# More block pairs by seven products in a decoder trunk, with weight sums made in DRAM by accumulating DMAs

## The chip, the cores and the metric

The kernel runs on one core of a Trainium2 chip. TensorE (PE) multiplies and adds up in PSUM; ScalarE (ACT), VectorE (DVE) and GpSimd (POOL) do elementwise work; SyncE (SP) issues DMAs, and ACT and POOL can issue them too. Sixteen DMA engines carry every transfer of the core. The metric is the device time of one execution in microseconds (us); lower is better.

## The reference

Everything is float32: a trunk of two layers over 256 tokens with a model width of 2048. Layer 0 is a retention mixer with eight heads, layer 1 a block-sparse attention with a relative position bias; a gated MLP with a causal convolution of width 3 follows each. Cut to what matters:

```python
for i in range(2):
    hn = rms_norm(h, mix_norm[i])
    if i == 0:                         # retention
        q, k, v, g = split(hn @ w_in)  # w_in 2048 x 12288: q, k 8 x 256, v, g 8 x 512
        ...
        h = h + (silu(g) * group_norm(o)) @ w_out      # 4096 x 2048
    else:                              # attention, T5 bias
        q, k, v = split(hn @ w_qkv)                    # 2048 x 6144
        h = h + attention(q, k, v) @ w_out             # 2048 x 2048
    u = causal_conv(rms_norm(h, ffn_norm[i]) @ w_up)   # 2048 x 11264
    gate, val = split(u)
    h = h + (silu(gate) * val) @ w_down                # 5632 x 2048
out = rms_norm(h, final_norm)
```

## The kernel before

**Precision.** A float32 value is kept as two parts of PE's faster float32 format, a high part and the rest. A product of two such values takes three matmuls: high by high, high by rest, rest by high. Activations stand transposed in SBUF, both parts side by side (hT, yT, oT, actT). Weights come from DRAM as float32 (tile raw, four buffers of 1 MB) and are split on the chip: ACT copies the high part to wh (L226), DVE subtracts to get the rest, wl (L227). wh and wl have four buffers each, of 1024 columns.

**Panels.** A list of "halves" is built first, and then run in order (`run`, `step`). A half is one split and the matmuls that use it. Before half i runs, the splits up to half i + 3 are issued (`LOOKAHEAD`), and the loads of raw up to two units beyond that (`issue_split`, `issue_dma`, on SP's queue). PE, ACT and DVE follow this program order; SP and POOL have their own. `panel_b` makes 256 columns transposed (q, k and the up projections): a unit of 1 MB is two halves. `panel_s` (L365) makes 1024 columns by pairs of 128 rows of the weight: a pair is a 2 x 2 block matrix, 256 tokens by 256 rows times 256 rows by 1024 columns, and one unit of 1 MB.

**Pairs by eight and by seven.** `eight` (L480) takes a pair as eight block products, which are 24 matmuls of 512 columns in two halves. `seven` (L450) takes it in the Strassen-Winograd form: seven products, 21 matmuls, in four halves of 6, 3, 6 and 6. It needs four sums of activation blocks ("forms") and four sums of weight blocks. The weight's sums are made by DVE in raw, in place, between the splits:

```python
def split_b11_b22(raw, wh, wl):          # L239
    b = blocks(raw)
    split_to(blocks(wh), blocks(wl), b[:, 0:4:3, :])
    dve.tensor_tensor(b[:, 0:2, :], b[:, 0:4:3, :], b[:, 1:2, :].to_broadcast([P, 2, 512]), op=ALU.add)
```

and `split_b21` (L244) adds two sums of 512 columns (L247, L248). The forms of a pair of the down projection are made in the up projection (`forms`, L1014), stored to DRAM (tile f, L1021) and fetched by ACT's queue (L440) into a slot of hT, eight slots in all; on arrival they are split by ACT and DVE (L445, L446). In the heads DVE makes them (`make_forms`, L412), once, and later heads use the same slots.

**Where it is used.** A string of letters per panel says which pair is taken how, A by eight and S by seven (L91 to L96). Each down projection has two panels of 22 pairs: ten by seven in the first (every second one from the fourth on) and eight in the second. A retention head is q, k (`panel_b`) and one panel of v and gate with eight pairs, three by seven (the last head two).

**Other pieces the change touches.** `rstd` (L580) ends in one POOL instruction (L583); in a head the scaling of the normed output waits for it (L852), and the transposes behind that (L545). `bias_skew` (L718) issues one DMA of 3 MB from DRAM to DRAM on ACT's queue; it is called in the second group of the first up projection, but its place in ACT's order is the scheduler's choice, and that is in head 1.

Of the kernel before, what the change touches and what calls it, by code (L numbers as in the profile page):

```python
# [14 lines left out]
ALU = mybir.AluOpType  # L15
# [53 lines left out]
def wide_seqs(first, second, n_slots=8):  # L69


    n = len(second)
    one = [(p, first.index(p) % n_slots if p in first else None, p in first) for p in range(n)]
    again = [(i % n_slots, p, False) for i, p in enumerate(first)][-n_slots:]
    again += [(again[i][0], p, True) for i, p in enumerate(first[:-n_slots])]
    again = again[: second.count("S")]
    others = [p for p in range(n) if p not in [q for _, q, _ in again]]
    two = []
    for c in second:
        slot, p, fresh = again.pop(0) if c == "S" else (None, others.pop(0), False)  # L80
        two.append((p, slot, fresh))
    return one, two


def head_seq(pairs, seq, fresh):

    again, others = list(enumerate(pairs)), [p for p in range(len(seq)) if p not in pairs]
    return [(*again.pop(0)[::-1], fresh) if c == "S" else (others.pop(0), None, False) for c in seq]
# [6 lines left out]
MOB_V_SEQ = head_seq([0, 2, 4], "AASASASA", True)  # L95
MOB_SEQS = wide_seqs([3, 5, 7], "AAASAAAA")  # L96


def build(tc, a, out):
# [53 lines left out]

    def issue_dma(u):
        src, n = units[u]
        raws[u] = wraw.tile([P, 2048], F32, name="raw")
        dst = raws[u].rearrange("p (c n) -> p c n", n=n)
        if len(src.shape) == 4:
            for b in range(2):
                nc.sync.dma_start(dst[:, :, b * 512 : (b + 1) * 512], src[:, :, b, :])  # L160
        elif u == 2:

            load_x(8, 12)
            nc.sync.dma_start(dst[:, :4], src[:, :4])
            load_x(12, 16)
            nc.sync.dma_start(dst[:, 4:], src[:, 4:])
        else:
            nc.sync.dma_start(dst, src)
        if u in consts:
            consts[u]()  # L170
# [68 lines left out]
    def split_b11_b22(raw, wh, wl):  # L239
        b = blocks(raw)  # L240
        split_to(blocks(wh), blocks(wl), b[:, 0:4:3, :])
        dve.tensor_tensor(b[:, 0:2, :], b[:, 0:4:3, :], b[:, 1:2, :].to_broadcast([P, 2, 512]), op=ALU.add)  # L242

    def split_b21(raw, wh, wl):  # L244
        b = blocks(raw)
# [41 lines left out]
    def emit(items):  # L287
        for unit, mms in items:
            units.append(unit)
            for hf, mm in enumerate(mms):  # L290
                emit_half(len(units) - 1, *(mm if isinstance(mm, tuple) else (hf, mm)))
# [71 lines left out]
        return hT[:, 2 * s, :], hT[:, 2 * s + 1, :]  # L363

    def panel_s(unit, xT, seq, temps, done, slots=hT_slot, end=None, before=None,  # L365
                stored=None):

# [24 lines left out]
        def mul(b, x, wh, wl):  # L392
            for xs, ws in ((x[0], wh), (x[0], wl), (x[1], wh)):
                n = count[b] = count.get(b, 0) + 1
                pe.matmul(acc[b], lhsT=xs, rhs=ws, start=(n == 1), stop=(n == uses[b]))  # L395
            if n == uses[b]:
                full.append(b)
# [52 lines left out]
        def seven(i, k, s):  # L450
            def b11_b22(wh, wl):
                opens(i)
                mul(1, xs(0, k), wh[:, 0, :], wl[:, 0, :])
                mul(3, fs(s, 3), wh[:, 1, :], wl[:, 1, :])
                give()

            def b21(wh, wl):
                mul(2, xs(0, k + 1), wh[:, 0, :], wl[:, 0, :])
                give()

            def u1_u3(wh, wl):
# [52 lines left out]

# [87 lines left out]
    def out_proj(w, seqs, xT, temps, g0, use_r, stored=None):  # L602
# [9 lines left out]
        emit(panel_s(unit_s(w, 0), xT, seqs[0], temps, residual_s(0, temps), stored=stored))  # L612
        emit(panel_s(unit_s(w, 1024), xT, seqs[1], temps,
                     residual_s(2, temps, lambda: [transpose_first(i) for i in range(2)], rest), stored=stored))

    def residual_s(j, temps, sevens_done=None, all_done=None, last=None):

# [98 lines left out]
        dma0(tblD, tbl[:AH])  # L716

    def bias_skew():  # L718
        dma0(skewD, bass.AP(tensor=tblD.tensor, offset=tblD.offset, ap=[[0, P], [1, AH * 3 * P]]))

    pools = {}

# [144 lines left out]
    def ret_head(hd):  # L867
        def k_done(acc):
            ret_qk("k")(acc)
            after(4, lambda: ret_scores(hd))  # L870

        def vg_done():
            after(3, lambda: ret_pv(hd))
            after(5, lambda: ret_yT(hd))
            if hd == 0:
                after(6, lambda: bias_load())
                after(8, lambda: bias_table())

        q = panel_b(w_in, hd * RDK, xT_h, ret_qk("q"), before=ret_begin if hd == 0 else None)
        k = panel_b(w_in, D + hd * RDK, xT_h, k_done)  # L880
        if hd == 0:
            emit_pairs(q, k)
        else:
            emit(q + k)

        def unit(k0):
            vg = w_in[k0 * P : (k0 + 2) * P, 2 * D :].rearrange("(c p) (b n) -> p c b n", p=P, b=2)
            return vg[:, :, :, hd * RDV : (hd + 1) * RDV], 1024

        def slots(s):  # L890

            c = (28, 30, 24, 26)[s]
            return yT[0][:, c, :], yT[0][:, c + 1, :]

        emit(panel_s(unit, xT_h, HEAD_SEQS[hd], make_temps(lambda: ret["p1"], af="bs", ff="m1"), ret_vg(vg_done), slots))
# [5 lines left out]
    for hd in range(RH):  # L901
        ret_head(hd)


# [84 lines left out]
    def ffn_layer(layer, begin, g_next, use_next, last):  # L989
# [3 lines left out]
        def stored(pair):  # L993
            return kept[pair]

        for j in range(NFB // 2):
            def gate_done(acc, j=j):
                if layer == 0 and j == 1:
# [24 lines left out]
            emit(panel_b(wu, j * 256, xT_h, gate_done, before=begin if j == 0 else None))  # L1023
            emit(panel_b(wu, DFF + j * 256, xT_h, val_done))
        if not last:
            return out_proj(wd, FFN_SEQS, actT, temps_ffn, g_next, use_next, stored)
# [7 lines left out]
        emit(panel_s(unit_s(wd, 0), actT, FFN_SEQS[0], temps_ffn, residual_s(0, temps_ffn), stored=stored))  # L1034
        emit(panel_s(unit_s(wd, 1024), actT, FFN_SEQS[1], temps_ffn, residual_s(2, temps_ffn, last=last_bank), end=4,
                     before=gains_first, stored=stored))

    def ffn_begin(prev):
        def f():
# [205 lines left out]
```

## Time and profile before

| what | value |
|---|---|
| time, median of 3 runs | 2559.3 us (2558.61 to 2559.44) |
| time of the profiled execution | 2559.53 us |
| its span, first to last instruction | 2557.4 us |
| mean granted clock of TensorE | 0.999 |
| DMA moved | 504.41 MB, mean 197 GB/s |
| DVE, ACT, POOL busy | 82%, 57%, 0% of the span |

Stages of the profiled execution, by the first use of their weights: retention heads to 535 us, its output projection to 707, up projection to 1196, down projection to 1427, attention to 1712, its output projection to about 1805, second up projection to 2290, second down projection to the end. The profile has a page, and views that answer questions on it: groups of instructions by line, waits, a timeline, windows (busy time by engine in a stretch, with the share of time that the 16 DMA engines were busy and the GB/s they moved). "Idle before" names what ended an engine's idle time. Matmuls are pipelined, so the time of one is longer than the distance to the next.

### The profile page before, as it was taken

The numbers are of one execution on the slowest core, as the hardware profiler recorded it, in microseconds if no ns is written. First come the engines' busy times: TensorE is split into PE (matmuls) and PEld (weight loads), VectorE is DVE, ScalarE is ACT, GpSimd is POOL, SyncE is SP. The second block draws the span as 40 slices with busy tenths as digits, with TensorE's granted clock in tenths as the row PEclk, the third lists the DMA queues.
The fourth block names the chain that finished last, engine by engine and source line by source line (L and its number), as shares of the span: only waits on it lengthen the run. The fifth ranks groups of instructions, "written<-read, shape, count | busy, mean of one in ns | idle before, by whom it ended". The sixth has DMA issues, their size and how long they took to land.

```text
span 2557.4 us, 34487 instructions
## 1 busy us (share of the span) xinstructions
PE 2545.5 (100%) x13277; PEld 2177.8 (85%) x13277; DVE 2107.6 (82%) x2766; ACT 1447.6 (57%) x1870; POOL 10.2 (0%) x24
## 2 busy tenths in 40 slices
PE   9999999999999999999999999999999999999998
PEld 8888888888888888888888888888888888888887
DVE  7888888998877777777898887768877777778997
ACT  6555555555565555555565655555655555555654
POOL 0000000000000000000000000000000000000000
PEclk9999999999999999999999999999999999999999
DMA  7665655555565656566665565555565656567654
GB/s 258 227 201 186 197 186 186 189 181 196 199 197 183 205 188 203 190 202 193 235 208 193 198 216 179 174 183 172 193 196 194 198 191 200 193 199 243 214 198 148
DMA packets 342196, 504.41 MB, mean 197 GB/s; under 512 B 9600, under 2 KB 260496, under 8 KB 341776
## 3 DMA queue, kind: packets, MB, share of 16 engines
q1 hardware_dynamic: 330672, 483.53, 57.2%
q10 hardware_dynamic: 11360, 18.69, 2.2%
q8 instruction: 104, 1.70, 0.3%
q14 instruction: 60, 0.49, 0.1%
HBM read 494.82 MB, written 10.51 MB: 198 GB/s over the span
## 4 chain that ended last, share of the span: by engine, by line
PE 95%; DVE 3%; ACT 1%; issue 1%; DMA 1%; SPq 0%; POOL 0%; POOLq 0%; ACTq 0%; DVEq 0%
PE acc L349 34%; PE aux L395 31%; PE acc L352 17%; PE acc L395 8%; DVE wl L227 1%; PE acc L315 1%; PE acc L317 1%; PE acc L316 1%; PE aux L529 0%; PE aux L528 0%; PE aux L527 0%; PE aux L545 0%; DMA raw<-in_ret_w_in_dram 0%; ACT wh L226 0%; PE acc L545 0%
## 5 line engine op out<-in xcount | busy, mean ns | idle before, releaser
L226 ACT ACTIVATE wh<-raw 128x1024 fp32r<-128x1024 f32 (+2 forms) x1067 | 1084.2, 1027 | 1005.4 <-PE acc L349 434.6
L227 DVE TENSOR_TENSOR wl<-raw,wh 128x1024 fp32r<-128x1024 f32 (+2 forms) x1067 | 1242.8, 1182 | 388.9 <-ACT wh L226 381.1
L349 PE MATMUL acc<-hT,wh 128*128 128x512 f32 x3840 | 1197.7, 393 | 1.0 <-DVE hT L551 0.8
L352 PEld LDWEIGHTS acc<-hT,wl 128*128 128x128 f32 x3840 | 720.4, 188 | 161.4 <-DVE wl L227 0.6
L352 PE MATMUL acc<-hT,wl 128*128 128x256 f32 x3840 | 761.3, 279 | 0.2 <-DVE wl L227 0.2
L349 PEld LDWEIGHTS acc<-hT,wh 128*128 128x128 f32 x3840 | 586.3, 188 | 3.0 <-ACT wh L226 1.6
L395 PE MATMUL aux<-wh,actT 128*128 128x512 f32 x976 | 319.3, 390 | 0.0
L395 PE MATMUL aux<-wh,hT 128*128 128x512 f32 x942 | 314.6, 390 | 0.4 <-ACT wh L226 0.2
L395 PEld LDWEIGHTS aux<-wh,actT 128*128 128x128 f32 x976 | 183.2, 188 | 38.6 <-DVE h L625 0.5
L395 PEld LDWEIGHTS aux<-wh,hT 128*128 128x128 f32 x942 | 176.7, 188 | 38.9 <-ACT wh L226 1.8
L395 PE MATMUL aux<-wl,actT 128*128 128x512 f32 x488 | 189.9, 389 | 0.0
L395 PE MATMUL aux<-wl,hT 128*128 128x512 f32 x471 | 183.8, 390 | 0.4 <-DVE wl L227 0.4
L934 DVE SCALAR_TENSOR_TENSOR t<-u,cw,t 128x256 f32<-128x256 f32 x352 | 146.7, 479 | 0.0
L395 PE MATMUL aux<-wh,yT 128*128 128x512 f32 x426 | 141.8, 391 | 0.4 <-ACT yT L226 0.4
L395 PE MATMUL acc<-wh,hT 128*128 128x512 f32 x358 | 131.6, 391 | 0.0
L395 PEld LDWEIGHTS aux<-wl,actT 128*128 128x128 f32 x488 | 91.6, 188 | 18.6
L395 PEld LDWEIGHTS aux<-wl,hT 128*128 128x128 f32 x471 | 88.4, 188 | 19.1 <-DVE wl L227 1.1
L395 PEld LDWEIGHTS aux<-wh,yT 128*128 128x128 f32 x426 | 80.0, 188 | 17.7 <-ACT yT L226 0.9
L930 ACT ACTIVATE t<-u,cw 128x256 f32<-128x256 f32 x176 | 94.9, 587 | 0.1
L242 DVE TENSOR_TENSOR raw<-raw 128x1024 f32<-128x1024 f32 x77 | 93.9, 1219 | 0.0
L395 PE MATMUL aux<-wl,yT 128*128 128x512 f32 x213 | 83.0, 390 | 0.0
L750 DVE TENSOR_TENSOR bs<-acc,bs 128x512 f32<-128x512 f32 x120 | 82.1, 684 | 0.0
(228 smaller groups left out, 1943.4 us busy)
## 6 DMA issues: line engine op xcount, KB each, us to landing
raw<-in_ffn_w_up_dram SPq DMA_DIRECT2D x176, 1024.0 KB, 5.1
raw<-in_ffn_w_down_dram SPq DMA_DIRECT2D x88, 1024.0 KB, 5.5
raw<-in_ret_w_in_dram SPq DMA_DIRECT2D x133, 512.0 KB, 4.7
raw<-in_moba_w_qkv_dram SPq DMA_DIRECT2D x48, 1024.0 KB, 5.3
raw<-in_ret_w_out_dram SPq DMA_DIRECT2D x32, 1024.0 KB, 5.5
raw<-in_ret_w_in_dram SPq DMA_DIRECT2D x29, 1024.0 KB, 5.7
raw<-in_moba_w_out_dram SPq DMA_DIRECT2D x16, 1024.0 KB, 5.4
f<-t ACTq DMA_DIRECT2D x20, 256.0 KB, 4.2
```

The source lines that it names most:

```text
L226: in_turn(act.activation(hi, src, AF.Copy))
L227: in_turn(dve.tensor_tensor(lo, src, hi.bitcast(F32), op=ALU.subtract))
L242: dve.tensor_tensor(b[:, 0:2, :], b[:, 0:4:3, :], b[:, 1:2, :].to_broadcast([P, 2, 512]), op=ALU.add)
L315: pe.matmul(acc, lhsT=xh, rhs=wh[:, c, :], start=(k == 0), stop=False)
L316: pe.matmul(acc, lhsT=xh, rhs=wl[:, c, :], start=False, stop=False)
L317: pe.matmul(acc, lhsT=xl, rhs=wh[:, c, :], start=False, stop=(k == nk - 1))
L349: pe.matmul(acc[:, b, :], lhsT=wh[:, c, b * P : (b + 1) * P], rhs=xt[:, k, :], start=(k == 0), stop=False)
L352: pe.matmul(acc[:, b, S:], lhsT=wl[:, c, b * P : (b + 1) * P], rhs=xt[:, k, :S], start=False, stop=(k == KC - 1))
L395: pe.matmul(acc[b], lhsT=xs, rhs=ws, start=(n == 1), stop=(n == uses[b]))
L750: dve.tensor_tensor(bs, acc[:, :, :S], bs, op=ALU.add)
L930: act.activation(t[:, i, :], u[:, i, 2:], AF.Identity, bias=c[:, 3, b : b + 1], scale=c[:, 2, b : b + 1])
L934: dve.scalar_tensor_tensor(t[:, i, :], u[:, i, tap : tap + S], c[:, tap, b : b + 1], t[:, i, :], op0=ALU.mult, op1=ALU.add)
```

## The change

1. **More pairs by seven.** Each down projection takes 24 of its 44 pairs by seven (18 before), twelve in each panel; five heads (2 to 6) take 4 of 8 (3 before). Per layer twelve forms are stored and sixteen fetched (ten and ten before): with eight slots, the second panel fetches four of them again.
2. **A third letter, P.** A P pair is by seven, but the sums of its weight blocks are read from DRAM. Its one unit of 1 MB becomes two: three plain blocks (0.75 MB, two DMAs) for the first two halves, and four sums (1 MB, tile wsum) for the last two. DVE adds nothing for it. Sixteen pairs in each down projection and two in each of the heads 2 to 6 are P: 42.
3. **Chains that make the sums** (`block_sums`). Two copies from DRAM to DRAM on ACT's queue put four plain blocks into wsum (1 MB); then POOL issues four accumulating DMAs of 256 KB: two at once onto the first two blocks, then one, then one more, each three halves behind the step before. The 42 chains are placed by hand in the stages before they are needed: a head's in the head before it; those of the first down projection in heads 6 and 7, the output projection and the up projection; those of the second in the attention, its output projection and the second up projection.
4. **`bias_skew`** keeps its place in program order, in the up projection.

```diff
 def wide_seqs(first, second, n_slots=8):
...
-    again = again[: second.count("S")]
+    again = again[: n - second.count("A")]
...
+def made_ahead(seq, letters):
+
+    return [p for (p, _, _), c in zip(seq, letters) if c == "P"]
...
-FFN_SEVENS = list(range(3, 22, 2))
-FFN_SEQS = wide_seqs(FFN_SEVENS, "AAASASASASASASASASAAAA")
-RET_SEQS = wide_seqs([5, 7, 9, 11, 13, 15], "AAASASASASASAAAA")
-HEAD_SEQS = [head_seq([0, 2, 4], "AASASASA", hd == 0) for hd in range(RH - 1)] + [head_seq([0, 2], "AASAASAA", False)]
...
+FFN_LETTERS = ("AAAPAPSAPAPSAPAPSAPAPS", "AAAPSPAPSPAPSPAPSPAAAA")
+FFN_SEQS = wide_seqs(*FFN_LETTERS)
+FFN_SEVENS = [p for p, slot, _ in FFN_SEQS[0] if slot is not None]
+RET_SEQS = wide_seqs("AAAAASASASASASAS", "AAASASASASASAAAA")
+HEAD_LETTERS = ["AASASASA"] * 2 + ["AAPSAPSA"] * 5 + ["AASAASAA"]
...
     def issue_dma(u):
         src, n = units[u]
+        src = src() if callable(src) else src
...
+        if isinstance(src, list):
+            for c, v in src:
+                nc.sync.dma_start(dst[:, c : c + v.shape[1]], v)
...
+    def split_front(raw, wh, wl):
+        split_to(wh[:, :512], wl[:, :512], raw[:, 1024:1536])
...
+            made = None if slot is None or sums is None else sums(pair)
+            mms = [(j, eight(i, j, k)) for j in range(2)] if slot is None else seven(i, k, slot, made)
+            mms = [(part, counted(mm)) for part, mm in mms]
+            if made is None:
+                items.append((unit(k), mms))
+                continue
+            items.append((made[0], [(0, mms[0][1]), (split_front, mms[1][1])]))
+            items.append((made[1], [(hf, mms[2 + hf][1]) for hf in range(2)]))
...
     def bias_skew():
-        dma0(skewD, bass.AP(tensor=tblD.tensor, offset=tblD.offset, ap=[[0, P], [1, AH * 3 * P]]))
+        tc.keep_in_program_order(dma0(skewD, bass.AP(tensor=tblD.tensor, offset=tblD.offset, ap=[[0, P], [1, AH * 3 * P]])))
...
+    def block_sums(name, w, n0, pairs, apart=512):
...
+        def add(dst, src):
+            tc.keep_in_program_order(nc.gpsimd.dma_start(dst, src, accum_op=ALU.add, max_dma_last_dim=8192))
+
+        def copies(pair):
+            s = summed[pair] = dram.tile([4, P, 512], F32, name="wsum")
+            for i in (0, 2):
+                c, step = ((0, P * n + apart), (0, P * n))[i // 2]
+                tc.keep_in_program_order(dma0(s[i : i + 2].rearrange("b p n -> p b n"), blk(pair, c, 0, step, 2)))
+
+        def first(pair):
+            for i in range(2):
+                add(summed[pair][i], blk(pair, 0, 1)[:, 0, :])
+
+        def second(pair):
+            add(summed[pair][2], summed[pair][1])
+
+        def third(pair):
+            add(summed[pair][3], summed[pair][2])
...
+    def place_chains(name, places):
+        while places and chains[name]:
+            at = places.pop(0)
+            for i, f in enumerate(chains[name].pop(0)):
+                later.append([at + 3 * i, f])
...
+    for hd in range(2, RH - 1):
+        place_chains(("head", hd), places((("head", hd - 1), 5, 12, 2)))
+    early = places((("head", 6), 5, 12, 2), (("head", 7), 5, 12, 2), ("ret_out", 6, 20, 3), ("up0", 8, 18, 9))
+    late = places(("moba", 8, 18, 5), ("moba_out", 6, 0, 1), ("up1", 8, 16, 10))
```

In `places` a stage's name is followed by the first half within it, the distance and the number of chains.

**PE, first down projection, seventh pair of the first panel.** Before, it is taken by eight (aux is a PSUM bank, wh and wl the split weight, actT the activations); these rows are its first 12 matmuls and one of the next:

```order
L395 MATMUL aux<-wh,actT 128x512
L395 MATMUL aux<-wl,actT 128x512
L395 MATMUL aux<-wh,actT 128x512 x2
L395 MATMUL aux<-wl,actT 128x512
L395 MATMUL aux<-wh,actT 128x512 x2
L395 MATMUL aux<-wl,actT 128x512
L395 MATMUL aux<-wh,actT 128x512 x2
L395 MATMUL aux<-wl,actT 128x512
L395 MATMUL aux<-wh,actT 128x512 x2
```

Now it is by seven, and its first two halves are these nine (hT holds the forms):

```order
L416 MATMUL acc<-wh,actT 128x512
L416 MATMUL acc<-wl,actT 128x512
L416 MATMUL acc<-wh,actT 128x512
L416 MATMUL aux<-wh,hT 128x512
L416 MATMUL aux<-wl,hT 128x512
L416 MATMUL aux<-wh,hT 128x512
L416 MATMUL aux<-wh,actT 128x512
L416 MATMUL aux<-wl,actT 128x512
L416 MATMUL aux<-wh,actT 128x512
```

Twelve matmuls have become nine; the second half of the pair has twelve in both. In the whole program PE has 51 matmuls of 128x512 fewer (17 pairs by three) and is otherwise the same.

**DVE, start of the first panel of the same down projection.** Before, each pair by seven has its three sums (raw<-raw) among the splits:

```order
L242 TENSOR_TENSOR raw<-raw 128x1024
L227 TENSOR_TENSOR wl<-raw,wh 128x512
L247 TENSOR_TENSOR raw<-raw 128x512
L248 TENSOR_TENSOR raw<-raw 128x512
L446 TENSOR_TENSOR hT<-hT 128x512
L227 TENSOR_TENSOR wl<-raw,wh 128x1024 x5
L227 TENSOR_TENSOR wl<-raw,wh 128x512
L242 TENSOR_TENSOR raw<-raw 128x1024
```

Now, from the first P pair to the first S pair (P A P S):

```order
L245 TENSOR_TENSOR wl<-raw,wh 128x512
L467 TENSOR_TENSOR hT<-hT 128x512
L245 TENSOR_TENSOR wl<-raw,wh 128x1024 x5
L245 TENSOR_TENSOR wl<-raw,wh 128x512
L467 TENSOR_TENSOR hT<-hT 128x512
L245 TENSOR_TENSOR wl<-raw,wh 128x1024 x2
L467 TENSOR_TENSOR hT<-hT 128x512
L245 TENSOR_TENSOR wl<-raw,wh 128x1024
L245 TENSOR_TENSOR wl<-raw,wh 128x512
L260 TENSOR_TENSOR raw<-raw 128x1024
L268 TENSOR_TENSOR raw<-raw 128x512
L269 TENSOR_TENSOR raw<-raw 128x512
```

The P pairs have splits alone; the sums stand only in the S pair.

**POOL, in the heads.** Before, POOL has nothing between one head's rstd and the next (the x8 is one per head):

```order
L679 MEMSET sums 128x2
L583 ISA
L583 TENSOR_TENSOR r<-v,sums 128x2
L704 MEMSET rbs 128x128
L583 TENSOR_TENSOR rs<-v,sums 128x2 x8
```

Now two chains stand between two of them (rs is the rstd of a head, wsum the sums in DRAM):

```order
L611 TENSOR_TENSOR rs<-v,sums 128x2
L897 DMA wsum<-in_ret_w_in_dram 128x512 x2
L897 DMA wsum<-wsum 32x2048 x2
L897 DMA wsum<-in_ret_w_in_dram 128x512 x2
L897 DMA wsum<-wsum 32x2048 x2
L611 TENSOR_TENSOR rs<-v,sums 128x2
```

Each add that reads what another DMA wrote waits on POOL for that DMA to land, and the rstd stands behind it.

More of the change, by code (lines that the diff above doesn't have):

```diff
@@ L144, in build @@
     halves = []
+    marks, chains = {}, {}
     state = {"dma": 0, "split": 0, "mm": 0}
@@ L365, in panel_s @@
     def panel_s(unit, xT, seq, temps, done, slots=hT_slot, end=None, before=None,
-                stored=None):
+                stored=None, sums=None):
         acc, count, uses, items, late = {}, {}, {}, [], []
@@ L448, in opens, with seven @@
                 make_forms(seq[i + 2][1], 2 * seq[i + 2][0])
-        def seven(i, k, s):
+        def seven(i, k, s, made):
             def b11_b22(wh, wl):
@@ L856, in ret_yT, with blk, units_of @@
         to_T(yT[0], 4 * hd, lambda t, c: y[:, t, c * P : (c + 1) * P], 64 + 4 * hd, 4)
+    def block_sums(name, w, n0, pairs, apart=512):
+        summed = {}
+        n = w.shape[1]
+        def blk(pair, c, b, step=0, count=1):
+            off = w.offset + (2 * pair + c) * P * n + n0 + b * apart
+            return bass.AP(tensor=w.tensor, offset=off, ap=[[n, P], [step, count], [1, 512]])
+        def add(dst, src):
[12 more added lines that the diff above has]
+            add(summed[pair][3], summed[pair][2])
+        def units_of(pair):
+            if pair not in pairs:
+                return None
+            plain = [(0, blk(pair, 0, 0, P * n + apart, 2)),
+                     (2, blk(pair, 1, 0))]
+            return (plain, 512), (lambda: summed[pair].rearrange("b p n -> p b n"), 512)
+        chains[name] = [[lambda f=f, p=p: f(p) for f in (copies, first, second, third)] for p in pairs]
+        return units_of
+    def place_chains(name, places):
[3 more added lines that the diff above has]
+                later.append([at + 3 * i, f])
+        assert not chains[name]
     xT_h = [hT]
@@ L893, in slots @@
             return yT[0][:, c, :], yT[0][:, c + 1, :]
-        emit(panel_s(unit, xT_h, HEAD_SEQS[hd], make_temps(lambda: ret["p1"], af="bs", ff="m1"), ret_vg(vg_done), slots))
+        emit(panel_s(unit, xT_h, HEAD_SEQS[hd], make_temps(lambda: ret["p1"], af="bs", ff="m1"), ret_vg(vg_done), slots,
+                     sums=block_sums(("head", hd), w_in, 2 * D + hd * RDV, made_ahead(HEAD_SEQS[hd], HEAD_LETTERS[hd]), RH * RDV)))
     ret_open()
@@ L901, in build @@
     for hd in range(RH):
+        marks["head", hd] = len(halves)
         ret_head(hd)
@@ L994, in stored @@
             return kept[pair]
+        sums_of = [block_sums(("down", layer, i), wd, 1024 * i, made_ahead(FFN_SEQS[i], FFN_LETTERS[i])) for i in range(2)]
         for j in range(NFB // 2):
@@ L1032, in gains_first @@
                     after(6 + 2 * j + t, lambda j=j, t=t: gain_final(j, t))
-        emit(panel_s(unit_s(wd, 0), actT, FFN_SEQS[0], temps_ffn, residual_s(0, temps_ffn), stored=stored))
+        emit(panel_s(unit_s(wd, 0), actT, FFN_SEQS[0], temps_ffn, residual_s(0, temps_ffn), stored=stored, sums=sums_of[0]))
         emit(panel_s(unit_s(wd, 1024), actT, FFN_SEQS[1], temps_ffn, residual_s(2, temps_ffn, last=last_bank), end=4,
-                     before=gains_first, stored=stored))
+                     before=gains_first, stored=stored, sums=sums_of[1]))
     def ffn_begin(prev):
@@ L1209, in moba, with mark, places @@
                 emit(panel_a(w_qkv, KC, 2 * D + g * 512, xT_h, v_done))
+    def mark(name):
+        marks[name] = len(halves)
+    mark("ret_out")
     out_proj(a["ret_w_out"][0], RET_SEQS, yT, make_temps(lambda: ret["p1"], af="bs", ff="m1", m="qT"), 32, lambda: make_rB(use_rB))
+    mark("up0")
     ffn_layer(0, ffn_begin("ret"), 16, lambda: make_rB(use_mob), False)
+    mark("moba")
     moba()
+    mark("moba_out")
     out_proj(a["moba_w_out"][0], MOB_SEQS, oT, make_temps(lambda: mob["p2"], af="qT0", ff="qT1", m="kT0"), 48, lambda: make_rB(use_rB))
+    mark("up1")
     ffn_layer(1, ffn_begin("mob"), None, None, True)
+    def places(*runs):
+        return [marks[name] + first + apart * i for name, first, apart, n in runs for i in range(n)]
+    for hd in range(2, RH - 1):
+        place_chains(("head", hd), places((("head", hd - 1), 5, 12, 2)))
+    early = places((("head", 6), 5, 12, 2), (("head", 7), 5, 12, 2), ("ret_out", 6, 20, 3), ("up0", 8, 18, 9))
+    late = places(("moba", 8, 18, 5), ("moba_out", 6, 0, 1), ("up1", 8, 16, 10))
+    for layer, p in enumerate((early, late)):
+        for i in range(2):
+            place_chains(("down", layer, i), p)
     run()
```

38 lines of the change are left out of this document (22 added, 16 removed).

## The prediction, made before the changed kernel ran

> **What bounds the kernel now.** I read the page first, busy time and the chain that ended last:
>
> ```profile
> PE 2545.5 (100%) x13277; PEld 2177.8 (85%) x13277; DVE 2107.6 (82%) x2766; ACT 1447.6 (57%) x1870; POOL 10.2 (0%) x24
> PE 95%; DVE 3%; ACT 1%; issue 1%; DMA 1%; SPq 0%; POOL 0%; POOLq 0%; ACTq 0%; DVEq 0%
> ```
>
> PE is busy for 2545.5 of 2557.4 us, so only 11.9 us are left to be won by better overlap; anything more must be PE work that goes. Next I read PE's waits, whose two longest are:
>
> ```profile
> PE aux L688 <- DVE ones L678: 1.1, 1, 1.1
> PE acc L349 <- DVE hT L551: 0.8, 1, 0.8
> ```
>
> In the whole run PE waits a microsecond here and there and never for a weight. So a matmul taken away is worth its full distance to the next, as long as ACT, DVE and the loads still keep ahead. That distance isn't the mean time that the groups give:
>
> ```profile
> L395 PE MATMUL aux<-wh,actT 128*128 128x512 f32 x976 | 319.3, 390 | 0.0
> 1315.23 0.62 PE L395 MATMUL aux<-wh,actT 128*128 128x512 f32 x2
> 1315.91 0.62 PE L395 MATMUL aux<-wh,actT 128*128 128x512 f32 x2
> 1315.00:1420.00 105.00, 105.00 (x464) 86.79 (x463) 95.56 (x102) 60.74 (x69) 0.00 (x0) 1.00 0.61 209
> ```
>
> One takes 390 ns, but two rows three matmuls apart start 0.68 us apart (timeline), and the window with nothing but such matmuls in a down projection has 464 in 105.00 us: **0.2263 us each**. (A window's columns are length, busy time of PE, PEld, DVE, ACT and POOL with counts, granted clock, share of DMA time, GB/s.)
>
> **The gain.** PE loses 51 matmuls of this form, three in each of 17 pairs (six per down projection in two layers, one in each of five heads). 51 x 0.2263 = 11.5 us. PE's other work is the same, so by this term alone the profiled execution's 2559.53 us become 2548.0. (That execution lies 0.2 us over the median, so no correction.)
>
> **Do ACT and DVE keep ahead?** Their prices, by form:
>
> ```profile
> L227 DVE TENSOR_TENSOR wl<-raw,wh 128x1024 fp32r<-128x1024 f32 x988 | 1194.0, 1222 | 388.9 <-ACT wh L226 381.1
> L226 ACT ACTIVATE wh<-raw 128x1024 fp32r<-128x1024 f32 x988 | 1035.4, 1059 | 973.1 <-PE acc L349 434.6 <-PE aux L395 192.9 <-issue 153.8
> L242 DVE TENSOR_TENSOR raw<-raw 128x1024 f32<-128x1024 f32 x77 | 93.9, 1219 | 0.0
> L227 DVE TENSOR_TENSOR wl<-raw,wh 128x512 fp32r<-128x512 f32 x78 | 53.4, 685 | 0.0
> L248 DVE TENSOR_TENSOR raw<-raw 128x512 f32<-128x512 f32 x77 | 53.2, 691 | 2.3
> L226 ACT ACTIVATE wh<-raw 128x512 fp32r<-128x512 f32 x78 | 49.4, 633 | 32.3 <-PE aux L395 18.0 <-PE acc L395 14.3
> L446 DVE TENSOR_TENSOR hT<-hT 128x512 fp32r<-128x512 f32 x20 | 13.7, 685 | 0.0
> ```
>
> - DVE on an A pair: 2 x 1.22 = 2.4 us, against 24 x 0.2263 = 5.4 us of PE. On an S pair with a fetched form: 3 x 1.22 + 0.69 for the splits, 1.22 + 2 x 0.69 for the sums (L247 taken as L248), 0.69 for the form: 7.6 us against PE's 4.8. On a P pair the sums fall away: 5.0.
> - Before, the first panel repeats A S: DVE 10.1 of PE's 10.2 us, and PE did not wait. Afterwards it repeats A P A P S: 2 x 2.4 + 2 x 5.0 + 7.6 = 22.6 of 111 x 0.2263 = 25.1 us, 90%. The second panel repeats P S P A: at most 20.1 of 19.7 if every form were fetched, 18.1 with none; four of its twelve are, which is some 18.8. The DVE is less pressed than before in the first, about equally in the second.
> - ACT: a P or S pair is 3 x 1.06 + 0.63, 3.8 us, 0.6 more with a form, against 4.8. The 84 copies that ACT issues are not on the trace; its nearest is the DRAM to DRAM copy of the skew at 562 ns in ACT's queue, so 84 x 0.56 = 47 us, or 2% of the span, on an engine at 57%. The new 512 splits (17) and forms (12) are 20 us more. All of it lies in ACT's idle time (the 973.1 us above, most of it waiting for PE). Without that cover each issue would cost at most 0.56 us.
>
> So I take **nothing** for these two.
>
> **The transfers.** This is the open part: the change moves more bytes.
>
> ```profile
> L719 ACTq DMA_DIRECT2D skewD<-tblD x1: 562/562/562, 114.6 to 114.6; - x1
> raw<-in_ffn_w_down_dram SPq DMA_DIRECT2D x88, 1024.0 KB, 5.5
> f<-t ACTq DMA_DIRECT2D x20, 256.0 KB, 4.2
> skewD<-tblD ACTq DMA_DIRECT2D x1, 3072.0 KB, 12.5
> SPq L168 <- DVE wl L227: 1869.8, 374, 13.8
> 14.00:38.00 24.00, 23.81 (x141) 20.63 (x140) 18.89 (x31) 18.43 (x35) 0.70 (x1) 1.00 1.05 382
> 1213.00:1228.00 15.00, 15.00 (x79) 12.81 (x79) 11.24 (x17) 9.06 (x12) 0.00 (x0) 1.00 0.97 324
> 110.00:130.00 20.00, 19.90 (x93) 16.14 (x93) 16.95 (x23) 9.97 (x12) 0.00 (x0) 1.00 0.79 270
> 200.00:263.00 63.00, 63.00 (x319) 53.63 (x318) 55.35 (x73) 33.38 (x41) 0.69 (x1) 1.00 0.59 188
> ```
>
> SP's queue spends 1870 us waiting for a raw buffer to come free: the loads wait for the splits, not the splits for the loads. The 16 engines give 324 to 382 GB/s when busy all the time (0.97 and 1.05 of the stretch), and in both of these PE lost 0.2 us at most. The fourth window holds the 3 MB skew copy beside a head's loads: 270 GB/s, PE at 19.90 of 20.00.
>
> - Down projection. 44 pairs of 1.05 MB, 16 P pairs with 0.79 MB more, 16 forms of 0.26 MB: 62.9 MB in 984 x 0.2263 = 222.7 us, **282 GB/s** on average (215 before by the same sum), and P S P A alone is 5.77 MB in 19.7 us, 293 GB/s. That is 75 to 90% of what the engines gave. It holds on average, with four buffers to even it out. Bounds: no loss if the engines give over 293, and if they give only 270 (the fourth window, which was not full) 62.9 / 0.270 = 233 us, or 10 us lost per layer. I take 0.5 us per layer, near the full windows.
> - Heads 2 to 6. 12.6 MB in 68 us before (the last row has 188 GB/s). Two P pairs add 1.57 MB, two chains 2.1 MB of copies and eight adds of 0.26 MB. An **accumulating add** is on no row. Below, one pass of 0.26 MB at 324 GB/s, 0.8 us of all engines; above, three passes (read, read, write), 2.4 us, or the whole 4.2 us to landing of a 256 KB store, if nothing overlapped. I take two passes, 1.6 us. Per chain and half a head (33.7 us): loads 7.1 MB are 21.9 us, copies 3.2, adds 4 x 1.6 = 6.5, together 31.6. It fits, at 94%. At 2.4 us per add it is 34.9, 1.2 us too much, ten times over: 12 us lost. At 4.2 us it is 41.9 and 82 us lost.
> - Up projections have one chain per 44 to 50 us on top of 195 GB/s. At 50 us the loads are 9.75 MB or 30 us, the chain 10: 40 of 50. Nothing lost. The skew copy moves there; it cost at most 0.1 us where it was, so it is worth 0 either way.
>
> **POOL's order.**
>
> ```profile
> 298.35 0.69 POOL L583 TENSOR_TENSOR rs<-v,sums 128x2 f32<-128x2 f32 x1 [67.37 <-DVE v L582]
> 299.07 0.88 DVE L852 TENSOR_SCALAR sg<-sg,rs 128x512 f32<-128x512 f32 x2 [0.22 <-POOL rs L583]
> 301.40 0.90 PEld L545 LDWEIGHTS aux<-laid,sg 128*128 128x128 f32 x8
> ```
>
> POOL now waits for landings, and behind it stands rs; behind rs DVE (L852, and all splits after it), and 1.6 us behind that PE's transposes. The head's last add is issued at half 26 of 32, rs falls at half 3 of the next head: nine halves, some 24 us, later, and the add's own landing isn't waited for. A chain's steps are three halves, 8 us, apart; the 256 KB store landed in 4.2. So rs comes in time unless the steps take over 20 us. I take 0, at worst the 5 us of two halves per head.
>
> Beside this stands the Trainium skill, "SBUF — State Buffer", the box on the "DVE blocks DMA" trap: while DVE runs a one-input float32 operation in its two-port mode, GpSimd can't write the descriptors of the DMAs it issues. The trace bears out such a mode only for L852 (two of 512 columns in 0.88 us, where two-input ones take 0.69 each); there are two per head, so by the rule an add starts under 1 us late, and the sum is the same by either.
>
> **Forecast.** 2548.0 + 1.0 = **2549.0 us**, 0.4% faster.
>
> **The rivals.**
>
> 1. *The down projection is bound by its loads.* SP's wait for buffers would vanish there and ACT wait for raw. For: 282 GB/s against 215, rows of 2 KB for the P units instead of 4, short halves (1.4 us) that make three halves of lead worth 4 us. Against: both full windows. The gain is eaten at 62.9 / (222.7 + 5.8) = 275 GB/s. At 278, 3.6 us per layer: 2555, within 0.2%. At 270: 2568.
> 2. *Slower than before: the adds cost more than two passes and the heads run out of DMA time.* Ten stretches of 33.7 us in heads 2 to 6; it decides at 1.2 us lost in each, 2.4 us per add. At 3 us an add: 37.1 us, 34 us lost, 2582. For: no row shows an add, and it must read its target before it writes. Against: four raw buffers, and copies that landed 3 MB in 12.5 us. Beside it, the Trainium skill, "DMA: Bandwidth & Descriptors", section "Latency and other measured facts": engines 7 and 15 are usually slower, by its guess because descriptor rings that GpSimd writes share their ports. No run here shows it; a load ends with its slowest engine, so by that rule loads beside the adds land later, in this rival's direction.
> 3. *POOL comes late in the heads* (steps over 20 us): 5 us in each of seven heads, 2549 + 35 = 2584.
> 4. *The change doesn't do what it says*: the sums cost PE as much as they save, since the short P halves leave splits too late; 0.68 us in each of 17 pairs, so 2559.
>
> **How the numbers follow.** Forecast (2546.5 to 2553) 0.62; rival 1 0.13, half of it still faster by over 0.2%; rival 2 0.14, a third of it below 2554; rival 3 0.04; rival 4 0.07. Under 2554.2 is faster by over 0.2% of the median, which is about what a measurement of this kernel tells from no change: 0.62 + 0.06 = 0.68. Same 0.15: rival 4 and the middle of rivals 1 and 2. Slower 0.17. Range: the low end is the whole gain with the ends of the program 1.5 us better; the high end is three passes per add with the loss of the down projections, 2549 + 12 + 2 = 2563.
>
> **What would show it.** PE 51 matmuls fewer at the same 0.226 us and busy near 2534; the down projections some 4 us shorter each, windows there near 280 GB/s; ACT without waits for raw; an add landing within 8 us; rs 68 us after the last. Wrong if ACT waits for loads of wsum or w_in, if POOL's rs is followed by a long wait of DVE, or if the heads' windows pass 320 GB/s with PE idle.

## The result, and the profile after

The changed kernel takes **2595.55 us** (median of 4 runs, 2593.05 to 2597.99) against 2558.98 us before (2558.61 to 2559.44): a ratio of 1.0143, interval 1.0128 to 1.0158. It is 36.6 us slower, where 10 us faster was forecast. The profiled execution took 2596.0 us, with a span of 2594.2.

From the page of the changed kernel, the busy times, the chain that ended last and the DMA queues; under them the longest waits of PE (total us, times, longest):

```profile
PE 2549.9 (98%) x13226; PEld 2167.4 (84%) x13226; DVE 2093.0 (81%) x2754; ACT 1474.4 (57%) x1917; POOL 146.4 (6%) x192
PE 86%; DVE 8%; ACT 3%; issue 1%; DMA 1%; POOL 0%; ACTq 0%; POOLq 0%; SPq 0%; DVEq 0%
q1 hardware_dynamic: 356176, 516.56, 59.7%
q0 software_dynamic: 16128, 44.05, 10.3%
q10 hardware_dynamic: 36512, 66.93, 8.8%
PE aux L416 <- ACT wh L244: 25.9, 27, 1.4
PE acc L416 <- ACT wh L244: 6.4, 17, 0.8
```

PE has its 51 matmuls fewer (13226 for 13277). But 44.3 us of the span are idle, for 11.9 before. DVE and ACT hold 11% of the chain (4% before) and DMA no more than it had. The new wait is for wh, ACT's high part of a weight, in the panels (L416), 44 times. A matmul that was held up is booked with up to 0.50 us in place of 0.39, so this row alone understates the loss; where it lies is seen from when each stage's loads are issued. These rows of SP's queue give, at their end, the first and the last issue; the first three are of before, the others of the changed kernel.

```profile
L168 SPq DMA_DIRECT2D raw<-in_ret_w_out_dram x32: 367/368/368, 535.1 to 704.5; - x32
L168 SPq DMA_DIRECT2D raw<-in_ffn_w_up_dram x176: 367/368/368, 707.0 to 2290.4; - x176
L168 SPq DMA_DIRECT2D raw<-in_moba_w_out_dram x16: 367/368/368, 1712.2 to 1805.1; - x16
```

```profile
L186 SPq DMA_DIRECT2D raw<-in_ret_w_out_dram x32: 367/368/368, 550.1 to 719.8; - x32
L186 SPq DMA_DIRECT2D raw<-in_ffn_w_up_dram x176: 367/368/3503, 722.3 to 2317.8; - x176
L186 SPq DMA_DIRECT2D raw<-in_moba_w_out_dram x16: 367/368/368, 1739.6 to 1832.5; - x16
```

| stretch | before | after | change | matmuls that went | lost |
|---|---|---|---|---|---|
| heads (to 535.1 / 550.1) | 535.1 | 550.1 | +15.0 | 15, or 3.4 us | 18.4 |
| retention's output projection | 171.9 | 172.2 | +0.3 | none | 0.3 |
| up projection, first down projection, attention | 1005.2 | 1017.3 | +12.1 | 18, or 4.1 us | 16.2 |
| attention's output projection, second up projection | 578.2 | 578.2 | 0.0 | none | 0.0 |
| the rest, above all the second down projection | 267.0 | 276.4 | +9.4 | 18, or 4.1 us | 13.5 |

The two stages that only carry chains lost 0.3 us and nothing. The three with P pairs lost 48.1 us. In them 26 S pairs stand right behind a P pair (ten in the heads, eight in each down projection), and 48.1 / 26 is 1.85 us each.

What happens at one of them is seen in the timeline (start, duration, then what waited in square brackets), in the first S pair of the first down projection. ACT, DVE and the last PE rows:

```profile
1262.98 1.06 ACT L244 ACTIVATE wh<-raw 128x1024 fp32r<-128x1024 f32 x1 [1.66 <-PE aux L416]
...
1264.07 1.23 DVE L245 TENSOR_TENSOR wl<-raw,wh 128x1024 fp32r<-128x1024 f32 x1 [1.49 <-ACT wh L244]
...
1265.21 0.68 DVE L467 TENSOR_TENSOR hT<-hT 128x512 fp32r<-128x512 f32 x1
...
1265.82 1.82 DVE L245 TENSOR_TENSOR wl<-raw,wh 128x1024 fp32r<-128x1024 f32 x2
...
1267.54 0.39 PE L416 MATMUL acc<-wh,actT 128*128 128x512 f32 x1
1267.56 1.22 DVE L260 TENSOR_TENSOR raw<-raw 128x1024 f32<-128x1024 f32 x1
...
1268.81 0.69 DVE L268 TENSOR_TENSOR raw<-raw 128x512 f32<-128x512 f32 x1
1268.87 1.06 ACT L244 ACTIVATE wh<-raw 128x1024 fp32r<-128x1024 f32 x1 [2.83 <-DVE raw L260]
...
1269.36 0.39 PE L416 MATMUL aux<-wh,actT 128*128 128x512 f32 x1
1269.53 0.69 DVE L269 TENSOR_TENSOR raw<-raw 128x512 f32<-128x512 f32 x1
1269.98 0.49 PE L416 MATMUL acc<-wh,hT 128*128 128x512 f32 x1 [0.24 <-ACT wh L244]
1270.14 3.62 DVE L245 TENSOR_TENSOR wl<-raw,wh 128x1024 fp32r<-128x1024 f32 x3
1270.32 2.95 ACT L244 ACTIVATE wh<-raw 128x1024 fp32r<-128x1024 f32 x3 [0.39 <-DVE raw L269]
1271.43 0.50 PE L416 MATMUL aux<-wh,actT 128*128 128x512 f32 x1 [0.95 <-ACT wh L244]
1271.77 0.40 PE L416 MATMUL acc<-wl,hT 128*128 128x512 f32 x1
```

Read it from PE's gaps upwards. PE could have begun the S pair's third half at 1269.59 (1269.36 + 0.23). It begins at 1269.98, when ACT's copy of the summed blocks is there (1268.87 + 1.06), and its next matmul comes at 1271.43. That one, of the fourth half, needs ACT's next copy, which started behind L269; the one behind it needs DVE's subtraction for the third half (1270.14 + 1.22 = 1271.36). Both end at once. The distances are 0.62, 1.45 and 0.34 us in place of 0.23 each: 1.73 us lost. Now the start: DVE is busy without a gap from 1264.07 on, so DVE began too late. What let it begin was PE's release of a wh buffer, for the last split of the P pair (ACT at 1262.98, behind a PE wait). With four wh buffers and splits three halves ahead, that split can't come sooner.

The same place before, an A pair ahead of the S pair; the last row is the third half's first matmul:

```profile
1272.81 0.63 ACT L226 ACTIVATE wh<-raw 128x512 fp32r<-128x512 f32 x1 [0.30 <-PE acc L395]
...
1274.57 1.22 DVE L242 TENSOR_TENSOR raw<-raw 128x1024 f32<-128x1024 f32 x1
...
1277.77 1.22 DVE L227 TENSOR_TENSOR wl<-raw,wh 128x1024 fp32r<-128x1024 f32 x1
...
1280.09 0.39 PE L395 MATMUL acc<-wh,hT 128*128 128x512 f32 x1
```

Here DVE's big sum starts 5.5 us ahead of the third half (2.4 us in the changed kernel) and the subtraction is done at 1278.99, 1.1 us before it. So the sum to make is that of the stretch between a buffer's release and the half that needs the result. With P ahead: from 1262.8 PE has the P pair's 21 matmuls and the S pair's first nine, 30 x 0.2263 = 6.8 us; ACT and DVE need 1262.8 to 1271.36, 8.6 us, for the P pair's last split, the form, and the S pair's first two splits, three sums and third split. 1.8 us are missing. With A ahead, from 1272.6, PE has 24 + 9 matmuls, 7.5 us, and the work was done after 6.4.

### The profile page after: what moved, and what is told of

The parts are those of the page before. It is cut to its first block, busy times and chain, and to the rows that moved or that the text cites. A ratio compares the mean times of both kernels' runs of the same rounds, so it can differ in the third digit from the quotient of the medians.

```text
span 2594.2 us, 35076 instructions
## 1 busy us (share of the span) xinstructions
PE 2549.9 (98%) x13226; PEld 2167.4 (84%) x13226; DVE 2093.0 (81%) x2754; ACT 1474.4 (57%) x1917; POOL 146.4 (6%) x192
## 3 DMA queue, kind: packets, MB, share of 16 engines
q1 hardware_dynamic: 356176, 516.56, 59.7%
q0 software_dynamic: 16128, 44.05, 10.3%
## 4 chain that ended last, share of the span: by engine, by line
PE 86%; DVE 8%; ACT 3%; issue 1%; DMA 1%; POOL 0%; ACTq 0%; POOLq 0%; SPq 0%; DVEq 0%
PE acc L370 34%; PE aux L416 25%; PE acc L373 17%; PE acc L416 6%; DVE wl L245 4%; ACT wh L244 3%; DVE raw L260 1%; DVE raw L268 1%; DVE raw L269 1%; DMA raw<-in_ffn_w_down_dram 1%; PE acc L336 1%; PE acc L338 1%; PE acc L337 1%; PE aux L573 1%; PE aux L557 0%
## 5 line engine op out<-in xcount | busy, mean ns | idle before, releaser
L244 ACT ACTIVATE wh<-raw 128x1024 fp32r<-128x1024 f32 (+2 forms) x1101 | 1106.1, 1020 | 969.4 <-PE acc L370 396.2
L245 DVE TENSOR_TENSOR wl<-raw,wh 128x1024 fp32r<-128x1024 f32 (+2 forms) x1101 | 1272.3, 1175 | 414.2 <-ACT wh L244 405.5
L416 PE MATMUL aux<-wh,hT 128*128 128x512 f32 x906 | 307.4, 392 | 9.9 <-ACT wh L244 9.7
L416 PE MATMUL aux<-wh,actT 128*128 128x512 f32 x832 | 279.1, 392 | 16.1 <-ACT wh L244 16.1
L416 PEld LDWEIGHTS aux<-wh,hT 128*128 128x128 f32 x906 | 170.0, 188 | 49.7 <-ACT wh L244 14.4
L416 PEld LDWEIGHTS aux<-wh,actT 128*128 128x128 f32 x832 | 156.3, 188 | 52.9 <-ACT wh L244 21.1
L416 PE MATMUL aux<-wl,hT 128*128 128x512 f32 x453 | 176.7, 390 | 0.4 <-DVE wl L245 0.4
L416 PE MATMUL acc<-wh,hT 128*128 128x512 f32 x440 | 164.1, 397 | 3.4 <-ACT wh L244 3.4
L416 PE MATMUL aux<-wl,actT 128*128 128x512 f32 x416 | 162.1, 390 | 0.0
L416 PE MATMUL aux<-wh,yT 128*128 128x512 f32 x436 | 145.8, 391 | 0.4 <-ACT yT L244 0.4
L897 POOL DMA_DIRECT2D wsum<-in_ffn_w_down_dram x64 | 53.5, 836 | 1037.9 <-DMA wsum<-in_ffn_w_down_dram 839.9
L416 PEld LDWEIGHTS acc<-wh,hT 128*128 128x128 f32 x440 | 83.0, 189 | 26.4 <-ACT wh L244 9.6
L416 PEld LDWEIGHTS aux<-wl,hT 128*128 128x128 f32 x453 | 85.0, 188 | 18.4 <-DVE wl L245 1.0
L416 PEld LDWEIGHTS aux<-wh,yT 128*128 128x128 f32 x436 | 81.8, 188 | 18.2 <-ACT yT L244 0.9
L416 PEld LDWEIGHTS aux<-wl,actT 128*128 128x128 f32 x416 | 78.2, 188 | 16.3
```

What stands on the lines that cost most here:

```text
L244: in_turn(act.activation(hi, src, AF.Copy))
L245: in_turn(dve.tensor_tensor(lo, src, hi.bitcast(F32), op=ALU.subtract))
L897: tc.keep_in_program_order(nc.gpsimd.dma_start(dst, src, accum_op=ALU.add, max_dma_last_dim=8192))
```

## The experiments

Three theories stood against each other: **lead** (an S pair right behind a P pair has not enough PE time ahead of it for its chain of sum, copy and subtraction), **transfers** (copies, adds and the larger loads make weights late), and **DVE's sum of work** (a group of pairs has too much of it, in whatever order). All are edits of the changed kernel, unless said otherwise; before stood at 2558.55 us in the first four, 2558.69 in the next two and 2558.84 in the last two.

**1. S ahead of P.** The pairs by seven and the chains in the same number; only the letters are swapped, so that no S pair follows a P pair.

```diff
-FFN_LETTERS = ("AAAPAPSAPAPSAPAPSAPAPS", "AAAPSPAPSPAPSPAPSPAAAA")
+FFN_LETTERS = ("AAAPASPAPASPAPASPAPASP", "AAASPPASPPASPPASPPAAAA")
-HEAD_LETTERS = ["AASASASA"] * 2 + ["AAPSAPSA"] * 5 + ["AASAASAA"]
+HEAD_LETTERS = ["AASASASA"] * 2 + ["AASPASPA"] * 5 + ["AASAASAA"]
```

> Only the order of letters differs: every P S becomes S P (the second panel's P S P becomes S P P), so each S pair has an A pair ahead of it again; counts of matmuls, DVE sums, chains and bytes are those of the changed kernel. Theory 'lead' (in an S pair the third split waits for DVE's sums, and only a long A pair ahead of it gives the splits enough lead; 26 S pairs lose some 1.8 us each): most of the 48 us comes back, 2550 to 2565 us, and PE no longer waits at the S pairs. Theory 'loads' (the down projections and heads are short of DMA time): unchanged within 5 us of 2595. Theory 'DVE's sum of work is too large per group': unchanged too, since its sum per group is the same.

Measured: 2555.69 us (2554.51 to 2557.27), ratio to before 0.9989 (0.998 to 0.9998): 39.9 us under the changed kernel. With the same matmuls, sums, chains and bytes, the order alone is worth that much; neither the transfers nor DVE's sum of work is the main cause.

**2. No chains.** The copies and adds are left out, and the P pairs read four plain blocks in place of the sums (so the products are of other numbers, the loads as many bytes).

```diff
-            return (plain, 512), (lambda: summed[pair].rearrange("b p n -> p b n"), 512)
+            return (plain, 512), ([(2 * c, blk(pair, c, 0, apart, 2)) for c in range(2)], 512)
...
-                later.append([at + 3 * i, f])
+                pass
```

> Left out: all copies and accumulating DMAs; the second unit of a P pair loads four plain blocks of the weight (1 MB) in place of the sums, so the output isn't the reference's. Everything on PE, ACT and DVE and the loads by SP stays. Theory 'lead': within 5 us of 2595. Theory 'chains take the DMA time of the heads': the heads get back their 18 us, 2577, and the down projections, where no chain runs, stay. Theory 'POOL or ACT is held up by the chains': 2577 as well.

Measured: 2591.84 us (2591.15 to 2594.75), 1.0131 (1.0116 to 1.0146). The windows of heads 2 to 6 (columns as in the prediction) for the changed kernel, the swap and the kernel without chains, in this order:

```profile
156.00:530.00 374.00, 361.43 (x1796) 302.00 (x1795) 316.59 (x411) 199.47 (x244) 37.59 (x47) 1.00 0.86 258
156.00:530.00 374.00, 374.00 (x1881) 318.08 (x1880) 331.53 (x436) 211.30 (x256) 39.92 (x50) 1.00 0.87 268
156.00:530.00 374.00, 362.26 (x1801) 303.07 (x1800) 314.57 (x412) 200.71 (x245) 4.15 (x6) 1.00 0.60 201
```

Without the chains the DMA engines fall from 0.86 to 0.60 of the time, and PE waits nearly as much: it is busy for 362.26 of 374 us, 0.8 more than with them. With them, and S ahead of P, PE doesn't wait at all at 268 GB/s. So the loss of the heads is lead. The chains have at most a small part in it: the whole kernel is 3.7 us under the changed one, and the ranges of the two overlap.

**3. No sums.** DVE's three sums of an S pair (L260, L268, L269) are left out; its last two halves multiply blocks that are not summed.

```diff
-        dve.tensor_tensor(b[:, 0:2, :], b[:, 0:4:3, :], b[:, 1:2, :].to_broadcast([P, 2, 512]), op=ALU.add)
-        dve.tensor_tensor(b[:, 3, :], b[:, 0, :], b[:, 3, :], op=ALU.add)
-        dve.tensor_tensor(b[:, 2, :], b[:, 3, :], b[:, 2, :], op=ALU.add)
```

> Left out: DVE's sums of weight blocks in S pairs (three instructions each, everywhere in the program), so the output isn't the reference's; loads and chains stay. Theory 'lead': the third split of an S pair no longer waits, so 2546 to 2552 us. Theory 'loads' or 'chains': over 2580.

Measured: 2545.64 us (2544.92 to 2546.12), 0.9948 (0.9933 to 0.9963), just under the range forecast for 'lead'. With all transfers and all P pairs in place, 49.9 us go with 2.6 us of DVE's work in each S pair (all 52 of them, not only the 26 behind a P). That agrees with the 48.1 of the table. What is left against before is 12.9 us, near the 11.5 of the 51 matmuls. This run alone can't tell lead from DVE's sum of work, which falls too; experiment 1 does.

**4. The chains alone.** The pairs as before, all 42 chains issued and their sums not read.

```diff
-FFN_LETTERS = ("AAAPAPSAPAPSAPAPSAPAPS", "AAAPSPAPSPAPSPAPSPAAAA")
+FFN_LETTERS = ("AAASASASASASASASASASAS", "AAASASASASASASASASAAAA")
...
-            if pair not in pairs:
-                return None
+            return None
```

> The pairs are taken as in the kernel before (18 of 44 by seven with S alone, three of eight in the heads), but all 42 chains run at their places and nobody reads their result. Theory 'lead': 2559 to 2563 us, the chains are hidden. Theory 'chains': 2575 or more, with the heads longer by over 10 us.

Measured: 2559.25 us (2558.66 to 2559.81), 1.0001 (0.9992 to 1.0011). 168 adds and 84 copies cost nothing where PE has its lead.

**5. The second panel spread.** The swap left some 7 us against the forecast. PE's waits were in the second panels, where S P P follow each other. This one mixes them more evenly, with the same counts.

```diff
-"AAASPPASPPASPPASPPAAAA"
+"AASPASPASPASPAPPAPPAAA"
```

> As e1_swap, but the second panel of each down projection is AASPASPASPASPAPPAPPAAA in place of AAASPPASPPASPPASPPAAAA: the same numbers of A, P and S, no two P pairs beside an S, and one closing A fewer. e1_swap still lost some 8 us against the sum of matmuls (2548), all of it in the two second panels, with ACT waiting for raw. Theory 'loads of P pairs in a row come late there': with one P per group for most of the panel these waits go, 2547 to 2552 us. Theory 'DVE stays short after S' (an S followed by P has no lead either): no better than e1_swap, 2554 to 2558.

Measured: **2551.51 us** (2550.79 to 2552.78), 0.9972 (0.9961 to 0.9983): faster than both kernels. The windows of the second panel and two of ACT's waits, first of the swap, then of this one:

```profile
1335.00:1440.00 105.00, 102.72 (x452) 82.79 (x451) 91.03 (x98) 67.47 (x81) 0.00 (x0) 1.00 0.79 280
ACT wh L244 <- DMA raw<-in_ffn_w_down_dram: 18.6, 14, 3.2
ACT wh L244 <- DMA raw<-wsum: 8.4, 6, 2.3
```

```profile
1335.00:1440.00 105.00, 104.73 (x464) 86.24 (x463) 92.83 (x98) 68.19 (x81) 0.00 (x0) 1.00 0.86 292
ACT wh L244 <- DMA raw<-in_ffn_w_down_dram: 4.4, 5, 1.9
ACT wh L244 <- DMA raw<-wsum: 3.9, 2, 2.4
```

Two P pairs in a row load 3.67 MB in the 9.5 us of their 42 matmuls, 386 GB/s, and ACT then waits for loads; spread, the engines move 292 GB/s and PE is busy for 104.73 of 105 us. The waits went together with the row of P pairs; no run changed the loads alone, so that they are the whole of the cause is argued and not shown.

**6. The heads back to P S**, the down projections as in the swap.

```diff
-HEAD_LETTERS = ["AASASASA"] * 2 + ["AASPASPA"] * 5 + ["AASAASAA"]
+HEAD_LETTERS = ["AASASASA"] * 2 + ["AAPSAPSA"] * 5 + ["AASAASAA"]
```

> As e1_swap, but the five heads again have P S (AAPSAPSA). Theory 'lead': the ten S pairs of the heads lose what they lost in the changed kernel, 18 us over e1_swap, 2574 us, with the loss in the heads alone. A theory by which the heads were slow for their chains or loads, which e1_swap has too, would leave it at 2556.

Measured: 2572.51 us (2570.23 to 2575.93), 1.0057 (1.0041 to 1.0072): 16.8 us for ten S pairs behind a P, 1.7 each.

**7. Less lead without any P pair.** The kernel before, with splits two halves ahead and three buffers of wh and wl.

```diff
-LOOKAHEAD = 3
+LOOKAHEAD = 2
-    whi = ctx.enter_context(tc.tile_pool(name="whi", bufs=4))
+    whi = ctx.enter_context(tc.tile_pool(name="whi", bufs=3))
-        wl = wlo[i % 4].tile([P, 1032], F32R, name="wl")[:, c0 : c0 + 1024]
+        wl = wlo[i % 3].tile([P, 1032], F32R, name="wl")[:, c0 : c0 + 1024]
```

> The kernel before, with its splits issued two halves ahead in place of three, and three buffers of wh and of wl in place of four: no P pair, no chain, the same work, one half less of lead. Theory 'lead' (an S pair's third split needs a DVE sum, an ACT copy and a DVE subtraction in a row, 1.22 + 1.06 + 1.22 us, and it costs PE whatever of that is not ahead of it): the third half of many of the 77 S pairs stalls, 0.3 to 1 us each, so 2580 to 2640 us, with PE waiting for wh and wl in the halves behind the sums. Rival (what costs is something of P pairs alone, their transfers or their four short halves, and lead does not matter): within 5 us of 2559.

Measured: 2621.47 us (2621.16 to 2622.92), 1.0247 (1.023 to 1.0264). Its timeline at an S pair behind an A pair, from the S pair's first matmul to the third half:

```profile
1306.73 0.39 PE L395 MATMUL acc<-wh,actT 128*128 128x512 f32 x1
...
1308.07 1.23 DVE L227 TENSOR_TENSOR wl<-raw,wh 128x1024 fp32r<-128x1024 f32 x1 [0.63 <-ACT wh L226]
...
1308.81 0.39 PE L395 MATMUL acc<-wh,hT 128*128 128x512 f32 x1
1309.35 0.50 PE L395 MATMUL acc<-wl,hT 128*128 128x512 f32 x1 [0.15 <-DVE wl L227]
...
1309.69 0.64 PE L395 MATMUL acc<-wh,hT 128*128 128x512 f32 x2
```

The third half waits for DVE's subtraction: 0.54 and 0.34 us in place of 0.23 each, 0.42 us lost, at an S pair that follows an A pair, and at nearly every one of this down projection the same. For 77 such pairs that is 32 us. It is only half of the 62.6 us. Part of the rest shows as a longer distance between matmuls that wait for nothing: nine from 1306.73 to 1308.81, 0.231 us each, for 0.226 before, at a granted clock of 1.00. In the first up projection, where no pair is taken by seven, the pace is as before (290 matmuls from 950 to 1000 us in both). Why is open. So the run shows that lead decides at S pairs, and its total isn't a measure of it.

**8. Two of the three sums later.** L268 and L269 are moved behind the split of the third half.

```diff
+    def split_u1_u3(raw, wh, wl):
+        b = blocks(raw)
+        split_to(wh, wl, raw[:, :1024])
+        dve.tensor_tensor(b[:, 3, :], b[:, 0, :], b[:, 3, :], op=ALU.add)
+        dve.tensor_tensor(b[:, 2, :], b[:, 3, :], b[:, 2, :], op=ALU.add)
```

(The two sums leave `split_b21` for it, and the third half is split by it.)

> The changed kernel, with DVE's two sums of 512 columns moved behind the split of an S pair's third half; the sum of 1024 columns stays where it was. Theory 'the chain of the first sum, ACT's copy and DVE's subtraction holds the third half': ACT's copy lies beside the two sums anyway, so the third half comes at most 0.2 us earlier and the fourth as much later: 2590 to 2610 us. Rival 'the two sums ahead of the subtraction hold the third half': 1.2 us less in each of 26 S pairs behind a P pair, about 2565.

Measured: 2595.73 us (2594.93 to 2598.28), 1.0146 (1.0131 to 1.0162), the same as the changed kernel. But the edit hardly reached DVE. These are its rows at the first S pair of the first down projection (L272 and L273 are the two sums in this kernel; the first of the three L245 is the subtraction of the third half):

```profile
1269.90 0.69 DVE L272 TENSOR_TENSOR raw<-raw 128x512 f32<-128x512 f32 x1
1270.62 0.69 DVE L273 TENSOR_TENSOR raw<-raw 128x512 f32<-128x512 f32 x1
1271.23 3.63 DVE L245 TENSOR_TENSOR wl<-raw,wh 128x1024 fp32r<-128x1024 f32 x3
```

Both sums still run ahead of the subtraction, as in the changed kernel, and so they do at 24 of the 26 S pairs behind a P pair; at the other two, one sum has moved. So within a pair DVE doesn't always keep the order in which the program writes its work, and the run decides nothing between the two theories, although the time lies in the range of the first. Whether another order of the sums would help is open.

More lead for the changed order (a fifth buffer of wh and wl) was not tried.

## Why the prediction was wrong

- **The gain, 51 x 0.2263 = 11.5 us: right, as far as the runs show.** Without the sums the kernel is 12.9 us under before, and with the spread order, which computes the same as before, 7.2 us.
- **"So I take nothing for these two" (ACT and DVE): this is the step that failed.** It compared DVE's work with PE's over a whole cycle of five pairs (22.6 of 25.1 us) and four (18.8 of 19.7). The sums were right, and DVE is busy for no more than before (81%). But what an A pair leaves over can't be saved up: four buffers let a split run three halves ahead and no more, and P's halves are short (0.68 to 1.36 us, for A's 2.72). Over the stretch that counts, from the release of the buffer for the P pair's last split to the S pair's third half, it was 8.6 of 6.8 us: 1.8 us short, 26 times. The runs show 1.85 (table), 1.7 (experiment 6) and, for all of it, 49.9 us (experiment 3).
- **Rival 4 had the mechanism, with a chance of 0.07, and the wrong size**: 0.68 us in each of 17 pairs. It priced one short half of the pair that changes; the price lies at the S pair behind it, whose chain is three instructions on two engines.
- **The transfers of the down projection: half right.** 282 GB/s on average can be carried (292 in experiment 5), and of the 48 us none was theirs. In the swap, though, with two P pairs in a row, ACT waited for loads, and PE lost some 7 us. The changed order has no two P pairs in a row.
- **The price of an add: right.** 10.3% of 16 engines over 2594.2 us, by 168 adds, is 1.59 us each; 1.6 was taken. The DMA share of the heads was 0.86, where 94% was worked out. Rival 2 did not come, although the time did end on its side.
- **POOL's order and the skew copy: right.** DVE's wait for POOL's rstd in the heads, and the window of the first up projection with its chains and the skew copy, in the changed kernel:

```profile
DVE sg L880 <- POOL rs L611: 1.8, 8, 0.2
710.00:1190.00 480.00, 480.00 (x2735) 420.05 (x2734) 373.61 (x513) 273.81 (x357) 27.50 (x36) 1.00 0.80 240
```

  Eight heads wait 0.2 us each for rs, as before, and PE is busy for all 480 us.
- **What was to show it wrong** named ACT's waits for loads, POOL's rs and windows over 320 GB/s. PE waiting for a split wasn't on the list.
- **Two slips that changed nothing.** Before, PE did wait for weights (wh or wl), five times and 1.2 us in all, where "never" stands. And the chance of "faster" (0.68) leaves out the third of rival 2 that lies below 2554, 0.05 more.

## What to carry to other kernels

An engine that keeps up on average can still be late: add up the feeding engines' work, with the latency of its longest chain, from the release of a buffer to the piece that needs the result (here 30 matmuls of PE), and do it for each pair of neighbours in the order. Work that becomes shorter gives its successor less lead, so a faster piece belongs behind the piece that needs the longest preparation, not ahead of it. And mix pieces that load much with pieces that load little, rather than two of a kind.

## What the runs showed of the hardware

**The granted clock fell to half after a short stall.** The windows of the changed kernel around the longest stall of its second panel, and under them one around another stall:

```profile
1397.00:1400.00 3.00, 2.76 (x13) 1.84 (x11) 2.97 (x4) 0.56 (x1) 0.00 (x0) 1.00 1.03 374
1400.00:1402.00 2.00, 0.49 (x1) 0.19 (x1) 1.92 (x4) 1.60 (x3) 0.00 (x0) 1.00 0.53 205
1402.00:1406.00 4.00, 4.00 (x11) 3.13 (x12) 3.48 (x4) 2.48 (x3) 0.00 (x0) 0.59 0.38 98
1403.00:1406.00 3.00, 3.00 (x9) 2.32 (x8) 2.48 (x4) 1.48 (x2) 0.00 (x0) 0.50 0.50 128
1406.00:1410.00 4.00, 4.00 (x19) 3.29 (x18) 3.01 (x3) 3.22 (x4) 0.00 (x0) 0.98 0.71 235
1350.00:1353.00 3.00, 1.32 (x5) 0.58 (x4) 3.00 (x5) 2.14 (x3) 0.00 (x0) 1.00 0.22 85
```

After one matmul in two microseconds the clock was 0.59 on average over four, and 0.50 over the last three of them (11 matmuls where 18 are usual, some 1.6 us lost), then nearly full again. Experiment 8 has the same behind the same stall (0.50 from 1404 to 1407 us). The other stall, with 1.7 of 3 us idle, left it at 1.00. What decides between them the runs don't show. The Trainium skill, "TensorE: Matmul & The Clock Gate", Part 1, has the clock go to half after at least one idle window of about 3.4 us; half the rate fits, but here PE was idle for no more than about 1.5 us of two, and at most 0.96 us in one piece (timeline).

**Accumulating DMAs from DRAM to DRAM**, from the profile's list of DMA issues of the changed kernel (count, KB each, median us to landing):

```profile
wsum<-wsum POOLq DMA_DIRECT2D x84, 256.0 KB, 5.6
wsum<-in_ffn_w_down_dram POOLq DMA_DIRECT2D x64, 256.0 KB, 5.7
skewD<-tblD ACTq DMA_DIRECT2D x1, 3072.0 KB, 18.9
```

An add of 256 KB lands in 5.6 us. A plain store of that size (f<-t) took 4.2 us before, and 6.2 in this kernel, where the DMA engines are busier, so the add is not the slower one. By the queues' rows an add takes 10.3% / 44.05 of the engines' time per MB, against 59.7% / 516.56 for the plain loads: twice as much. The skew copy, which now lies beside the up projection's loads and chains, took 18.9 us for 12.5.
